# A two-layer hybrid encoder on one core: products moved from GpSimd to VectorE, later transposes and SSD matmuls, and another layer boundary

## The chip, the core and the metric

The kernel runs on one core of a Trainium2 chip. The core has five engines with queues of their own: TensorE (PE in the profile; its weight loads are PEld), VectorE (DVE), ScalarE (ACT), GpSimd (POOL) and SyncE (SP), which here only issues DMAs. The metric is the time of one execution on the device in microseconds (us), the median of the runs; lower is better.

## The reference

A sequence of 272 tokens (16 learned tokens and 256 frames) of width 2048 passes two layers, each followed by a residual and a layer norm:

```
for layer in range(2):
    f = even_mixer(h) if layer % 2 == 0 else odd_mixer(h)
    h = layer_norm(4 ** 0.25 * h + f, ln_g[layer], ln_b[layer])
```

Layer 0 projects `h` once, runs four heads of gated linear attention (GLA) and eight heads of stick-breaking attention beside each other, gates each with a Silu, and projects back. Layer 1 is a Mamba-2 mixer: a projection to z (4096), x (4096), B and C (1024 each) and dt (64); a causal convolution of four taps and a Silu over x, B and C; and per group g (8 groups of 8 heads)

```
xdt   = x * softplus(dt_raw + dt_bias)
l_mat = exp(a_cum[t] - a_cum[s]) where s <= t, else 0     # per head
cb    = C B^T                                             # per group
y     = (l_mat * cb) @ xdt + d_skip * x                   # the state between chunks included
y     = rms_norm(y * silu(z)) * norm_w
```

and a projection back. All inputs and the output are float32.

## The kernel before

Activations stand transposed: 128 features on the partitions, 272 tokens along the row, 16 such blocks (`kt`). Weights stream in as units of 1 MB (`raw`). ScalarE rounds each half unit to `whi`, an engine subtracts to get `wlo` (`split_into`, L145 to L147; VectorE, or POOL for one in six late in layer 1), and a product of float32 quality takes three matmuls: `whi` with `xhi`, `whi` with `xlo`, `wlo` with `xhi` (L165 to L167). A projection unit is 48 of them, a half unit 24. `whi` and `wlo` have five buffers of half a unit, `raw` three of a whole one; `pj` is a PSUM tile for projections (four buffers), `po` one for everything else (two), and `zb` are two fixed ones (`z`).

The mixers are Python generators ("side tasks"), which advance by one `yield` whenever the main loop ticks, four times a projection unit. That is the order in which the program is written. A list scheduler then reorders the instructions of each engine by its own estimate of times; only data dependencies hold, unless the program pins instructions. On the chip each engine runs its list in that order.

The places that the change touches:

- Stick-breaking heads (`post_sq`, `post_sk`, `post_sv`, `mix_sb`): one unit each for q, k, v of a head; the mixer is pushed at v.
- The last units of layer 0 (`out0c_unit`, c = 4 to 7), with `stat0` for each finished block of `hacc`: `xhi`/`xlo` of it times `ln_g`, and its sum and sum of squares, on POOL for blocks 0 to 13, as extra matmuls ("spare") for 14 and 15.
- `norm0`: the dt projection of 64 columns (48 matmuls into `po`), the sums over partitions by matmuls with `ones`, and mean and 1/deviation (`newton`).
- `first1`: the first six units of layer 1 (B, C, z, x, x, x of group 0) run on the rows before normalization; `fix` corrects each result by the mean and 1/deviation. Meanwhile `normalize0` normalizes `hacc`, and `residual1` transposes it into `acc` (L942, L943). After them `xhi`/`xlo` are written anew (L920, L921).
- `dt_path`: softplus of dt, the scan along the tokens (`dt_scr`, L976), a write to memory (`edr`) from which each group reloads 1.7 MB of broadcast rows (`ebc`), and transposes (`est`).
- Per group: `decay1` (M = exp of differences, L1054 to L1057; C B^T, L1069; M times it, L1080), `x_path` (Silu, transposes L1117 and L1121, times dt, `xd`), and `mix_ssd` (L1176, L1182). `silu1` clamps on VectorE (L1006), takes Exp, Ln and Exp on ScalarE (L1007 to L1009) and multiplies on POOL (L1010).
- SP's list holds the weight loads, `edr` and `ebc`, each waiting for its turn.

## Time and profile before

| | us |
|---|---|
| median of 3 runs | 1405.14 (1403.98 to 1405.44) |
| the profiled execution | 1403.88 |
| its span, first to last instruction | 1402.2 |
| PE busy | 1378.8 (98%) |
| VectorE busy | 1031.1 (74%) |
| ScalarE busy | 770.0 (55%) |
| POOL busy | 320.0 (23%) |

Layer 0 fills the span up to about 690 us. A row of the timeline gives start, length, engine, line and operation, and in brackets the idle time of the engine just before it with what ended that. A row of a group gives the busy time of all its instructions and the mean of one in ns. `L` numbers are lines of the kernel before. A fp32 matmul shows as two records.

### The profile page before, as it was taken

The numbers are of one execution on the slowest core, as the hardware profiler recorded it, in microseconds if no ns is written. First come the engines' busy times: TensorE is split into PE (matmuls) and PEld (weight loads), VectorE is DVE, ScalarE is ACT, GpSimd is POOL, SyncE is SP. The second block draws the span as 40 slices with busy tenths as digits, with TensorE's granted clock in tenths as the row PEclk, the third lists the DMA queues.
The fourth block names the chain that finished last, engine by engine and source line by source line (L and its number), as shares of the span: only waits on it lengthen the run. The fifth ranks groups of instructions, "written<-read, shape, count | busy, mean of one in ns | idle before, by whom it ended". The sixth has DMA issues, their size and how long they took to land. (4 is left out here: it accounts for less than half of the span.)

```text
span 1402.2 us, 26134 instructions
## 1 busy us (share of the span) xinstructions
PE 1378.8 (98%) x10719; PEld 1328.2 (95%) x10719; DVE 1031.1 (74%) x1669; ACT 770.0 (55%) x1144; POOL 320.0 (23%) x285
## 2 busy tenths in 40 slices
PE   9999999999999999999999999999999999999996
PEld 8999999999999999999999899899898999989985
DVE  7857575575565574558799989777887778777787
ACT  6645454354345544545587766655555655556551
POOL 0000100100101100114302325333323433424233
PEclk9999999999999999999999999999999999999998
DMA  9545444545454445443444745554646456464551
GB/s 331 178 154 171 161 160 171 172 160 179 153 179 153 153 153 194 160 153 137 151 151 172 265 170 194 202 208 162 218 157 227 176 185 225 155 210 177 193 197 61
DMA packets 37720, 249.84 MB, mean 178 GB/s; under 512 B 4256, under 2 KB 6112, under 8 KB 9184
## 3 DMA queue, kind: packets, MB, share of 16 engines
q1 hardware_dynamic: 37168, 247.77, 50.6%
q8 instruction: 84, 1.38, 0.4%
q10 hardware_dynamic: 432, 0.39, 0.1%
q14 instruction: 36, 0.29, 0.1%
HBM read 245.94 MB, written 2.20 MB: 177 GB/s over the span
## 5 line engine op out<-in xcount | busy, mean ns | idle before, releaser
L165 PE MATMUL pj<-xhi,whi 128*128 128x272 f32 (+4 forms) x2560 | 733.6, 287 | 1.1 <-ACT xhi L317 0.7
L166 PE MATMUL pj<-xlo,whi 128*128 128x272 f32 (+4 forms) x2560 | 731.1, 286 | 0.0
L167 PE MATMUL pj<-xhi,wlo 128*128 128x272 f32 (+4 forms) x2560 | 729.5, 285 | 0.0
L147 DVE TENSOR_TENSOR wlo<-raw,whi 128x1024 fp32r<-128x1024 f32 (+2 forms) x405 | 510.4, 1263 | 239.5 <-ACT whi L146 237.7
L146 ACT ACTIVATE whi<-raw 128x1024 fp32r<-128x1024 f32 (+2 forms) x435 | 449.8, 1038 | 392.5 <-PE pj L166 337.4
L165 PEld LDWEIGHTS pj<-xhi,whi 128*128 128x128 f32 x2560 | 482.2, 188 | 3.9 <-issue 1.0
L166 PEld LDWEIGHTS pj<-xlo,whi 128*128 128x128 f32 x2560 | 482.2, 188 | 1.7 <-issue 0.6
L167 PEld LDWEIGHTS pj<-xhi,wlo 128*128 128x128 f32 x2560 | 482.5, 188 | 0.8 <-issue 0.6
L165 PE MATMUL pj<-mixh,whi 128*128 128x272 f32 x384 | 110.9, 290 | 1.0 <-ACT mixh L801 1.0
L167 PE MATMUL pj<-mixh,wlo 128*128 128x272 f32 x384 | 110.4, 288 | 0.0
L166 PE MATMUL pj<-mixl,whi 128*128 128x272 f32 x384 | 110.4, 288 | 0.0
L147 POOL TENSOR_TENSOR wlo<-raw,whi 128x1024 fp32r<-128x1024 f32 x30 | 75.6, 2520 | 113.3 <-ACT whi L146 113.0
L476 PE MATMUL pj<-whi,yh 128*128 128x512 f32 (+1 forms) x244 | 94.8, 389 | 0.0
L478 PE MATMUL pj<-whi,yl 128*128 128x512 f32 (+1 forms) x244 | 94.2, 386 | 0.0
L477 PE MATMUL pj<-wlo,yh 128*128 128x512 f32 (+1 forms) x244 | 94.1, 386 | 0.0
L248 POOL TENSOR_TENSOR gr<-gr,gsc 128x1088 f32<-128x1088 f32 x6 | 15.4, 2569 | 302.1 <-ACT gsc L247 302.1
L165 PEld LDWEIGHTS pj<-mixh,whi 128*128 128x128 f32 x384 | 72.2, 188 | 1.3 <-ACT mixh L801 1.1
L166 PEld LDWEIGHTS pj<-mixl,whi 128*128 128x128 f32 x384 | 72.3, 188 | 0.2
L167 PEld LDWEIGHTS pj<-mixh,wlo 128*128 128x128 f32 x384 | 72.3, 188 | 0.1
L485 DVE SCALAR_TENSOR_TENSOR acc<-pj,rr,acc 128x512 f32<-128x512 f32 (+1 forms) x65 | 46.7, 735 | 12.1 <-PE pj L478 12.0
L478 PEld LDWEIGHTS pj<-whi,yl 128*128 128x128 f32 x244 | 45.8, 188 | 9.3
L476 PEld LDWEIGHTS pj<-whi,yh 128*128 128x128 f32 x244 | 45.8, 188 | 9.0
(327 smaller groups left out, 1527.4 us busy)
## 6 DMA issues: line engine op xcount, KB each, us to landing
raw<-in_wts SPq DMA_DIRECT2D x212, 1024.0 KB, 4.8
ebc<-edr SPq DMA_DIRECT2D x8, 1664.0 KB, 6.3
raw<-in_wts SPq DMA_DIRECT2D x9, 256.0 KB, 5.6
hacc<-in_xT SPq DMA_DIRECT2D x7, 272.0 KB, 5.7
early<-in_wts SPq DMA_DIRECT2D x2, 512.0 KB, 7.4
lg<-in_lnr SPq DMA_DIRECT2D x1, 1024.0 KB, 4.6
lb<-in_lnr SPq DMA_DIRECT2D x1, 1024.0 KB, 4.6
out_h<-acc SPq DMA_DIRECT2D x2, 512.0 KB, 2.6
```

The source lines that it names most:

```text
L146: self.nc.scalar.activation(hi, src, AF.Copy)
L147: eng.tensor_tensor(lo, src, hi.bitcast(F32), op=ALU.subtract)
L165: mm(ps, whi, xhi, start=first, stop=False)
L166: mm(ps, whi, xlo, start=False, stop=False)
L167: mm(ps, wlo, xhi, start=False, stop=last)
L248: mul(c, c, e, op=ALU.mult)
L476: mm(ps, yh[:, kk, tt], hi[:, k, :], start=kk == 0, stop=False)
L477: mm(ps, yh[:, kk, tt], lo[:, k, :], start=False, stop=False)
L478: mm(ps, yl[:, kk, tt], hi[:, k, :], start=False, stop=kk == 3)
L485: self.nc.vector.scalar_tensor_tensor(a, ps, r[:, t : t + 1], a, op0=ALU.mult, op1=ALU.add)
```

## The change

It has seven parts.

1. The mixer of a stick-breaking head is pushed at its k unit instead of its v unit; it waits for v's transposes only before the product with v.
2. The dt weights are loaded two units earlier and split one or two units earlier, into tiles of the v buffers in which high and low parts stand beside each other as 128 columns. The dt product then takes one matmul with `xhi` and one with `xlo` for each of 16 blocks, and a matmul with two stacked identities (`add2`) later sums the two halves.
3. `norm0` puts the sums of POOL ahead of the dt matmuls and the spare ones behind the tenth block, pins these on PE, subtracts the mean there (two blocks of `hacc` in one instruction), and splits the second unit of layer 1 itself. `keep_order` holds VectorE and ScalarE to the written order from the unit c = 6 to the end of `norm0`.
4. `normalize0` has only the scaling left, two blocks in one instruction. `dt_path` starts when `first1` has written `xhi`/`xlo` anew, instead of after 16 ticks.
5. The products of Silu of x (all groups) and of B and C (group 0), and all products of M with C B^T, are on VectorE; before, POOL had Silu's and two of four products of M in groups 2 to 7.
6. C B^T is held by two ticks (from group 1 on), x's transposes by five, SSD's matmuls by three, and each of these blocks is pinned on PE.
7. `split_half` skips what is already split.

The diff, cut to its core ("..." where lines are left out):

```diff
+    def keep_order(self, first):
+        ins = self.traced()
...
+        for eng in (mybir.EngineType.DVE, mybir.EngineType.Activation):
+            mine = [i for i in ins[n0:] if i.engine == eng]
+            for a, b in zip(mine, mine[1:]):
+                self.tc.add_manual_dep(b, a.name, free, reason="keep_order")
...
         if u[2] == 6:
-            self.dt_raw = self.lp.tile([P, 1024], F32, tag="gu", name="dtraw")
-            self.nc.sync.dma_start(self.dt_raw, self.wdt)
-        if u[2] == 7:
-            self.dt_parts = self.split(self.dt_raw, 1024)
+            self.first = self.traced()[-1]
+        if u[2] == 4:
+            self.dt_raw = self.lp.tile([P, 2, 8, 64], F32, tag="gu", name="dtraw")
+            self.nc.sync.dma_start(self.dt_raw.rearrange("p a k c -> p (a k c)"), self.wdt)
+        if u[2] == 5:
+            self.dt_parts = [self.lp.tile([P, 8, 2, 64], F32R, tag=n, name="dt" + n, bufs=2) for n in ("gvh", "gvl")]
+            for a, p in enumerate(self.dt_parts):
+                self.split_into(self.dt_raw[:, a], p[:, :, 0, :], p[:, :, 1, :], self.nc.vector)
...
     def post_sk(self, ps, h, j):
-        self.cur["k"] = self.sb_parts(ps, ("ke", "gk")[h % 2], 1.0)
+        k = self.sb_parts(ps, ("ke", "gk")[h % 2], 1.0)
+        v = self.cur["sv", h] = self.v_tiles(h)
+        self.mixers[4 + h // 4].append(self.push(self.mix_sb(h, self.cur["q"], k, v)))
...
     def norm0(self):
+        pin(mm(pm[:, :T], self.ones, self.ssum, start=True, stop=False))
+        pin(mm(pq[:, :T], self.ones, self.ssq, start=True, stop=False))
         for k in range(KT):
-            self.in_kt(self.ps_dt[:64, :TG], hi[:, k, :], lo[:, k, :], k, 0, TG)
...
+            if k == 10:
+                for n, (x, q) in enumerate(self.spare):
+                    l = n == len(self.spare) - 1
+                    pin(mm(pm[:, :T], self.ones, x, start=False, stop=l))
+                    pin(mm(pq[:, :T], self.ones, q, start=False, stop=l))
+            w = self.dt_parts[k // 8][:, k % 8].rearrange("p a c -> p (a c)")
+            pin(mm(self.ps_dt[:, :TG], w, self.xhi[:, k, :], start=k == 0, stop=False))
+            pin(mm(self.ps_dt[:, :TG], w, self.xlo[:, k, :], start=False, stop=k == KT - 1))
+        self.split_half(len(L0) + 1, 0)
...
+        center((0, 2))
         self.newton(rs, var, tmp)
...
+        self.split_half(len(L0) + 1, 1)
+        center(range(4, KT, 2))
+        self.keep_order(self.first)
...
     def dt_path(self, ps, scr):
-        for _ in range(16):
+        while not self.normed:
             yield
...
-    def silu1(self, v):
+    def silu1(self, v, eng=None):
-        self.nc.gpsimd.tensor_tensor(v, v, c, op=ALU.mult)
+        (eng or self.nc.gpsimd).tensor_tensor(v, v, c, op=ALU.mult)
...
     def decay1(self, g):
-        self.silu1(bc)
+        self.silu1(bc, None if g else vec)
...
+        for _ in range(2 if g else 0):
+            yield
         zb = self.zbank()
...
-            eng = nc.gpsimd if g > 1 and h in (2, 6) else vec
-            eng.tensor_tensor(M[:, h : h + 2, :], M[:, h : h + 2, :], c, op=ALU.mult)
+            vec.tensor_tensor(M[:, h : h + 2, :], M[:, h : h + 2, :], c, op=ALU.mult)
...
     def x_path(self, g, j):
-        self.silu1(xt[:, j : j + 2, :].rearrange("p a t -> p (a t)"))
+        self.silu1(xt[:, j : j + 2, :].rearrange("p a t -> p (a t)"), vec)
...
+        for _ in range(5):
+            yield
...
     def mix_ssd(self, g):
             if j == 0:
+                for _ in range(3):
+                    yield
```

How the scheduler's lists move, at three places. First PE at the end of the dt product, where `po_8046` and `po_8048` hold it and `pj_8138` and `pj_8143` are the first unit of layer 1. Before:

```order
L166 MATMUL po_8046<-xlo,whi_7976 64x274
L167 MATMUL po_8046<-xhi,wlo_7977 64x274
L165 MATMUL po_8046<-xhi,whi_7976 64x274
L848 MATMUL po_8095<-ssum,ones 128x272
L852 MATMUL po_8095<-hacc,ones 128x272
L166 MATMUL po_8046<-xlo,whi_7976 64x274
L167 MATMUL po_8046<-xhi,wlo_7977 64x274
L852 MATMUL po_8095<-hacc,ones 128x272
L165 MATMUL pj_8138<-xhi,whi_7980 128x274
```

With the change (the sums `ssum` and `ssq` stand ahead of the first dt matmul, and these rows follow the tenth block):

```order
L876 MATMUL po_8048<-xlo,dtgvl 128x274
L872 MATMUL z_64<-hacc,ones 128x272
L873 MATMUL z_65<-nsq_8029,ones 128x272
L872 MATMUL z_64<-hacc,ones 128x272
L178 MATMUL pj_8143<-xhi,whi_7982 128x274
L179 MATMUL pj_8143<-xlo,whi_7982 128x274
L180 MATMUL pj_8143<-xhi,wlo_7983 128x274
L178 MATMUL pj_8143<-xhi,whi_7982 128x274
L873 MATMUL z_65<-nsq_8046,ones 128x272
L875 MATMUL po_8048<-xhi,dtgvl 128x274
L876 MATMUL po_8048<-xlo,dtgvl 128x274
L875 MATMUL po_8048<-xhi,dtgvl 128x274
```

Block 14 and 15's `xhi` were read right behind each other at the end; now the spare sums and four rows of the next unit stand between.

Second, VectorE in group 3 around the second pair of x blocks (`xcl` is Silu's buffer, `gz` is z, `po_11355` and `po_11409` hold transposes). Before:

```order
L999 SCALAR_TENSOR_TENSOR xt_11059<-pj_11225,cpk,xt_11059 128x271
L999 SCALAR_TENSOR_TENSOR xt_11059<-pj_11225,cpk,xt_11059 128x270
L999 SCALAR_TENSOR_TENSOR xt_11059<-pj_11225,cpk,xt_11059 128x269
L1006 TENSOR_SCALAR xcl_11309<-xt_11059 128x544
L1130 TENSOR_TENSOR xd_11060<-po_11355,est 128x256 x2
L147 TENSOR_TENSOR wlo_11443<-raw_11371,whi_11442 128x1024
L147 TENSOR_TENSOR wlo_11477<-raw_11371,whi_11476 128x1024
L1130 TENSOR_TENSOR xd_11060<-po_11356,est 128x256 x2
L1136 TENSOR_TENSOR xd_8126<-z_64,est_8602 16x128 x4
```

With the change:

```order
L1044 SCALAR_TENSOR_TENSOR xt_11032<-pj_11196,cpk,xt_11032 128x271
L1044 SCALAR_TENSOR_TENSOR xt_11032<-pj_11196,cpk,xt_11032 128x270
L1044 SCALAR_TENSOR_TENSOR xt_11032<-pj_11196,cpk,xt_11032 128x269
L1051 TENSOR_SCALAR xcl_11282<-xt_11032 128x544
L160 TENSOR_TENSOR wlo_11394<-raw_11330,whi_11393 128x1024
L1055 TENSOR_TENSOR xt_11032<-xt_11032,xcl_11282 128x544
L160 TENSOR_TENSOR wlo_11444<-raw_11330,whi_11443 128x1024
L160 TENSOR_TENSOR wlo_11482<-raw_11390,whi_11481 128x1024
L1051 TENSOR_SCALAR xcl_11423<-gz_11328 128x512
L1180 TENSOR_TENSOR xd_11033<-po_11409,est 128x256 x2
L1180 TENSOR_TENSOR xd_11033<-po_11410,est 128x256 x2
L1186 TENSOR_TENSOR xd_8126<-z_64,est_8751 16x128 x4
```

The product of Silu now stands in VectorE's list behind its clamp and one weight split.

At the same place PE: before, the second pair's transposes stand 98 rows behind the end of the last x unit, one row into a z unit.

```order
L165 MATMUL pj_11373<-xhi,whi_11327 128x256
L166 MATMUL pj_11373<-xlo,whi_11327 128x256
L167 MATMUL pj_11373<-xhi,wlo_11328 128x256
L165 MATMUL pj_11441<-xhi,whi_11374 128x256
L1117 MATMUL po_11356<-ident,xt_11059 128x128 x4
L1121 MATMUL z_64<-ident,xt_11059 16x128 x2
L166 MATMUL pj_11441<-xlo,whi_11374 128x256
L167 MATMUL pj_11441<-xhi,wlo_11375 128x256
```

With the change, both pairs' stand together, 108 rows behind it:

```order
L179 MATMUL pj_11392<-xlo,whi_11333 128x256
L180 MATMUL pj_11392<-xhi,wlo_11334 128x256
L1167 MATMUL po_11409<-ident,xt_11032 128x128 x4
L1167 MATMUL po_11410<-ident,xt_11032 128x128 x4
L1171 MATMUL z_64<-ident,xt_11032 16x128 x4
L178 MATMUL pj_11392<-xhi,whi_11333 128x256
L179 MATMUL pj_11392<-xlo,whi_11333 128x256
```

The first pair's transposes have moved by one z unit. In groups 2, 4, 5, 6 and 7 the second pair's now stand 157, 125, 117, 109 and 125 rows behind that unit.

Third, PE at the first SSD matmuls of group 0 (`M_8677` and `M_8820` are M, `pj` x units of group 1). Before:

```order
L166 MATMUL pj_9238<-xlo,whi_9160 128x272
L1176 MATMUL po_9086<-M_8677,xd_8510 64x256 x2
L167 MATMUL pj_9238<-xhi,wlo_9161 128x272
L165 MATMUL pj_9238<-xhi,whi_9160 128x272
L166 MATMUL pj_9238<-xlo,whi_9160 128x272
L167 MATMUL pj_9238<-xhi,wlo_9161 128x272
L165 MATMUL pj_9238<-xhi,whi_9160 128x272
L166 MATMUL pj_9238<-xlo,whi_9160 128x272
L167 MATMUL pj_9238<-xhi,wlo_9161 128x272
L165 MATMUL pj_9238<-xhi,whi_9160 128x272
L1176 MATMUL po_9086<-M_8677,xd_8510 64x256 x2
L1176 MATMUL po_9086<-M_8677,xd_8510 64x144 x4
```

With the change:

```order
L178 MATMUL pj_9282<-xhi,whi_9246 128x272
L1167 MATMUL po_8951<-ident,xt_8482 128x128 x4
L1171 MATMUL z_64<-ident,xt_8482 16x128 x4
L1229 MATMUL po_9125<-M_8820,xd_8483 64x256 x4
L179 MATMUL pj_9282<-xlo,whi_9246 128x272
L180 MATMUL pj_9282<-xhi,wlo_9247 128x272
L178 MATMUL pj_9282<-xhi,whi_9246 128x272
```

Before they stand in the first x unit of group 1, in five pieces; now in the second, behind the transposes of the second pair, in two pieces.

## The prediction

> **What bounds the kernel now.** I read the page's first part, then PE's waits, then the timelines around them.

> ```profile
> span 1402.2 us, 26134 instructions
> ...
> PE 1378.8 (98%) x10719; PEld 1328.2 (95%) x10719; DVE 1031.1 (74%) x1669; ACT 770.0 (55%) x1144; POOL 320.0 (23%) x285
> ```

> PE is busy for all but 23 us, and part of that lies at the two ends of the program. So only two things can shorten the span: less work on PE, or fewer of PE's waits. All its waits are these nine:

> ```profile
> engine line waited for: us in total, times, longest us
> PE po L1117 <- POOL xt L1010: 4.4, 6, 1.1
> PE po L1176 <- DVE M L1080: 1.9, 1, 1.9
> PE po L165 <- ACT xhi L815: 1.3, 2, 0.7
> PE po L942 <- ACT acc L943: 1.2, 1, 1.2
> PE po L227 <- POOL b_one L217: 1.1, 1, 1.1
> PE pj L165 <- ACT mixh L801: 1.0, 1, 1.0
> PE pj L165 <- ACT xhi L317: 0.7, 1, 0.7
> PE pj L165 <- DVE fix L900: 0.3, 1, 0.3
> PE po L166 <- DVE xlo L816: 0.2, 1, 0.2
> ```

> Two of them (L227, L317: 1.8 us) belong to the start, which is left alone. The other seven, 10.3 us, all stand where the edits are. One costs more than its length. PE's timeline at the wait of 1.9 us (start, length, instruction), and three stretches of 1 us behind it (length, busy time of PE, PEld, DVE, ACT and POOL, granted clock of PE, DMA share, GB/s):

> ```profile
> 772.42 0.88 PE L1176 MATMUL po<-M,xd 128*64 128x256 f32 x4 [1.87 <-DVE M L1080]
> ...
> 774.08 0.43 PE L167 MATMUL pj<-xhi,wlo 128*128 128x272 f32 x1
> 774.30 0.43 PE L165 MATMUL pj<-xhi,whi 128*128 128x272 f32 x1
> ...
> 773.00:774.00 1.00, 1.00 (x5) 0.77 (x4) 1.00 (x2) 0.97 (x2) 0.00 (x0) 0.50 0.99 359
> 774.00:775.00 1.00, 1.00 (x7) 1.00 (x5) 1.00 (x3) 1.00 (x2) 0.00 (x0) 0.50 0.98 359
> ...
> 776.00:777.00 1.00, 1.00 (x13) 0.67 (x10) 1.00 (x3) 0.35 (x2) 0.77 (x1) 0.94 0.97 393
> ```

> PE looks busy there, but two projection matmuls start 0.22 us apart (774.08, 774.30), where 0.13 is usual (680.34 and 680.47, below). The granted clock tells why: it is 0.50 from about 772.7 to 776.7, and 4 us at half speed lose 2.0 us. This wait therefore costs 3.9 us.

> **The change part by part.** The profiled execution took 1403.9 us with its span of 1402.2; the median of the runs is 1405.1, so 1.2 us is added at the end. I call 680.34, where PE starts the dt matmuls, the boundary.

> ```profile
> 680.34 0.29 PE L165 MATMUL po<-xhi,whi 128*64 128x274 f32 x1
> 680.47 0.29 PE L166 MATMUL po<-xlo,whi 128*64 128x274 f32 x1
> ...
> 684.20 1.21 DVE L147 TENSOR_TENSOR wlo<-raw,whi 128x1024 fp32r<-128x1024 f32 x1
> 685.33 0.77 DVE L462 TENSOR_TENSOR hacc<-hacc,pj 128x272 f32<-128x272 f32 x2
> ...
> 688.68 0.62 PE L852 MATMUL po<-hacc,ones 128*128 128x272 f32 x2
> ...
> 695.42 0.43 DVE L860 SCALAR_TENSOR_TENSOR var<-po,ntmp 128x272 f32<-128x272 f32 x1
> ...
> 751.69 1.14 DVE L976 TENSOR_TENSOR_SCAN dt_scr<-dt_scr 64x272 f32<-64x272 f32 x3
> ...
> 758.38 1.60 DVE L1006 TENSOR_SCALAR xcl<-xt 128x544 f32<-128x544 f32 x1
> ...
> 764.60 0.94 DVE L1054 TENSOR_SCALAR M<-ebc,est 128x256 f32<-128x256 f32 x1 [2.48 <-DMA ebc<-edr]
> ```

> *Stick-breaking from the k unit.* The last head's values matmuls end 28 PE rows before the first matmul that reads its `mixh`, against none before: 28 x 0.125 = 3.5 us, over two operations of some 0.45 us each. Of 1.0 I take 0.9.

> *The boundary's waits.* The last two additions to `hacc` (L462) run at 685.33 though their matmuls ended by 680.3: VectorE is in order and has weight splits ahead of them (684.20). That makes `xhi` and `xlo` late, 1.5 us in all. Now the addition and `xlo` of both blocks stand together, with the dt split moved ahead, and PE has the two sums and 20 dt matmuls (3 us) before it needs them. The spare matmuls follow in the middle. All of the 1.5 goes.

> *The dt product.* 48 matmuls become 32, and starts are 0.125 apart (680.34, 680.47): -2.0. The sum over the two halves is one fp32 matmul, which PE runs as two passes (L852 at 688.68: two in 0.62, each 0.39 long, so 0.23 apart): +0.5. Net -1.5.

> *VectorE from the boundary on.* It is full there, so it decides how much of PE's gain remains. Unit prices (mean of one; starts in a row are 0.07 to 0.1 closer):

> ```profile
> L147 DVE TENSOR_TENSOR wlo<-raw,whi 128x1024 fp32r<-128x1024 f32 x390 | 502.0, 1289 | 237.2 <-ACT whi L146 235.7 <-issue 0.2
> ...
> L927 DVE TENSOR_TENSOR hacc<-hacc,z 128x272 f32<-128x272 f32 x16 | 5.7, 422 | 0.0
> ...
> L1006 DVE TENSOR_SCALAR xcl<-xt 128x544 f32<-128x544 f32 x16 | 9.4, 588 | 0.2
> ...
> L385 DVE SCALAR_TENSOR_TENSOR hacc<-hacc,shiftc 128x544 f32<-128x544 f32 x8 | 5.2, 719 | 0.0
> ...
> L318 DVE TENSOR_TENSOR xlo<-hacc,xhi 128x544 fp32r<-128x544 f32 x7 | 4.9, 723 | 0.0
> ```

> From L860 to the end of the scans VectorE needed 57.4 us (695.42 to 752.83). The rows of the change between the same two instructions: 16 centring and scaling operations of 544 columns instead of 32 of 272 (5.2/8 each against 5.7/16: -1.0), one weight split more (+1.1), seven convolution and two fix operations fewer at some 0.4 each, one small sum more (-3.3). That gives 54.2. `var` can start 5.3 us after the boundary (PE's sums and dt matmuls, then two ScalarE copies), so the scans end at 59.5. Walking PE's rows the same way (dt and sums 5.9; units of 48 at 0.12 to 0.13; transposes 0.11 each), it reaches the transposes of the scan at 59.4. The same addition for the two transposes of group 0's x: PE 83 and 95, VectorE 80.9 and 92.1, where both silu products of x (0.65 each) and that of B now lie on VectorE. VectorE is level or 2 to 3 us ahead, but collisions with POOL can eat that (L1006 at 758.38 took 1.60, where its mean is 0.59). No wait of M is left: M ends 10 us before PE asks, as the reload of `ebc` (2.48 us of waiting at 764.60) starts after 62 with no weights ahead of it in SP's queue.

> So the wait at L1176 with its half clock (3.9) goes, and up to 0.8 us comes back at the scan's or x's transposes: I take 3.1 (bounds 0 to 3.9). Of the waits at the residual's transposes and at L900 (1.5) I take 0.8 (0 to 1.5): ScalarE has the same row of copies there, and PE arrives earlier.

> [...]

> *Groups 2 to 7.* Six times PE waits for x's silu product on POOL. In group 3, and as groups:

> ```profile
> L1010 POOL TENSOR_TENSOR xt<-xt,xcl 128x544 f32<-128x544 f32 x16 | 24.9, 1557 | 86.5 <-ACT xcl L1009 86.5
> ...
> L1080 POOL TENSOR_TENSOR M<-M,cb 128x800 f32<-128x800 f32 x12 | 28.8, 2420 | 0.0
> ...
> L1080 DVE TENSOR_TENSOR M<-M,cb 128x800 f32<-128x800 f32 x20 | 37.2, 1894 | 6.8 <-POOL cb L236 6.7
> ...
> 772.54 0.97 DVE L1080 TENSOR_TENSOR M<-M,cb 128x800 f32<-128x800 f32 x1
> ...
> 960.53 1.04 DVE L1006 TENSOR_SCALAR xcl<-xt 128x544 f32<-128x544 f32 x1
> ...
> 964.16 0.65 ACT L1009 ACTIVATE xcl<-xcl 128x544 f32<-128x544 f32 x1
> ...
> 964.89 1.58 POOL L1010 TENSOR_TENSOR xt<-xt,xcl 128x544 f32<-128x544 f32 x1 [3.62 <-ACT xcl L1009]
> ```

> The product costs 0.72 on VectorE (as L318) instead of 1.56, and the second pair's transposes stand 108 to 157 PE rows behind the last x unit instead of 98 in group 3: 1 to 7 us more room. M's products cost 0.97 when POOL has none beside them, so four on VectorE take 3.9 us, where two took 3.8 (2 x 1.894) with POOL's 4.8 behind them. VectorE gets 16 x 0.72 of silu and loses about that by fewer collisions; it stays near its 74% of the span, and that is cover enough, since it idles 235.7 us in waits for `whi`. Of 4.4 I take 4.0. What comes next is the transposes of `xd`, 110 PE rows before the SSD matmuls: 13 us, no wait. Held SSD rows end long before the output units two groups later.

> *Pins.* SSD of group 0 goes in two pieces instead of five. At a return the first two projection starts lose some 0.1 us each: 0.4 (0 to 0.9).

> Sum: 0.9 + 1.5 + 1.5 + 3.1 + 0.8 + 4.0 + 0.4 = 12.2. 1403.9 - 12.2 + 1.2 = **1393 us**.

> **The rivals.**
> *A, VectorE swallows the boundary.* If its queue runs some 10 us later than I added up at x's second transposes, PE waits 7 us there and the terms from the boundary's waits to the residual's (6.9) are lost: 1393 + 6.9 = 1400. For it: VectorE has no slack here,

> ```profile
> 700.00:760.00 60.00, 58.45 (x481) 57.44 (x481) 59.89 (x131) 46.90 (x84) 5.38 (x5) 1.00 0.44 154
> ```

> Against: the addition by the same prices gives the old trace's 57.4 to 0.1. Chance 0.15.
> *B, the six waits stay,* because the transposes of groups 3 and 6 move by only some 10 rows, and the product now queues behind a weight split: 1397. Against: ScalarE's last exponential no longer stands behind VectorE's late clamp. Chance 0.12.
> *C, one new wait of 1.9 us or more* halves the clock again: 1393 + 3.9 = 1397. Likeliest at x's first transposes. Chance 0.10.
> *D, slower: VectorE blocked in order.* The product stands directly behind its clamp in groups 4 and 7, so VectorE idles through three ScalarE steps (about 2 us) while splits queue. A half unit is 24 matmuls, 3 us, and a split 1.3, so PE waits only if splits are less than 2 us ahead; at 14 such places it would be up to 28 us, 1409 if half of it shows. It decides from 0.9 us a place (12.2/14). Against: splits wait for PE (235.7 us on `whi`), not the reverse. Chance 0.05. [...]

> **How the numbers follow.** The forecast has 0.58. All gains whole give 14.7: 1390.5. My range is 1390 to 1400, which leaves out some 0.05 below, A with B together (gain 5.3 - 4.0 = 1.3: no change, 0.06 taken from A and B) and D. About 0.2%, 2.8 us, is what can be told here: faster 0.89, same 0.06, slower 0.05.

> **What would show it.** In the new profile PE's waits should be under 4 us in all, with none on POOL's `xt`, none on M, none on `xhi` behind the stick-breaking output, and the granted clock 1.00 from 700 to 800. Waits at the scan's or x's transposes of 1 to 2 us would show VectorE level with PE (my margin), 4 us and more rival A. The dt matmuls should be 32, 0.125 apart. It is wrong if PE waits on `wlo`, or if waits on `xt` merely change their engine.

## The result, and the profile after

| | before | with the change |
|---|---|---|
| median of six runs, us | 1404.9 | 1394.2 |
| lowest to highest, us | 1403.98 to 1405.44 | 1393.15 to 1394.98 |
| span of the profiled execution, us | 1402.2 | 1392.3 |

The ratio of the times is 0.9923, 95% interval 0.9913 to 0.9934: 10.7 us faster. The forecast was 1393, with a range of 1390 to 1400.

The page of the changed kernel, its first rows:

```profile
span 1392.3 us, 26070 instructions
...
PE 1376.1 (99%) x10705; PEld 1327.7 (95%) x10705; DVE 1014.6 (73%) x1684; ACT 771.3 (55%) x1146; POOL 261.9 (19%) x256
```

All of PE's waits in the changed kernel (line waited at, what was waited for, us in total, times, longest):

```profile
PE pj L178 <- DVE fix L935: 2.0, 1, 2.0
PE po L240 <- POOL b_one L230: 1.1, 1, 1.1
PE pj L178 <- ACT xhi L330: 0.6, 1, 0.6
PE z L867 <- POOL ssq L857: 0.4, 1, 0.4
PE pj L178 <- ACT whi L159: 0.4, 2, 0.2
PE po L987 <- ACT acc L988: 0.3, 1, 0.3
```

The span is 9.9 us shorter. PE's waits fell from 12.1 us to 4.8, which is 7.3, and its busy time from 1378.8 to 1376.1, which is 2.7: together 10.0. Gone are the waits for `mixh` (1.0), for `xhi` and `xlo` at the boundary (1.5), for M (1.9) and for x's Silu product (4.4). The wait at the residual's transposes shrank from 1.2 to 0.3. New are 0.4 for a sum of squares on GpSimd, 0.4 for rounded weights at the program's start, and one that no step of the prediction has: 2.0 us for a `fix`, the operation that takes an early layer-1 unit out of its `pj` tile in PSUM (a buffer for such a tile is called a bank below) and applies the norm. In PE's timeline of the changed kernel:

```profile
734.60 0.28 PE L180 MATMUL pj<-xhi,wlo 128*128 128x272 f32 x1
736.86 0.38 PE L178 MATMUL pj<-xhi,whi 128*128 128x256 f32 x1 [1.97 <-DVE fix L935]
...
737.20 0.28 PE L180 MATMUL pj<-xhi,wlo 128*128 128x256 f32 x1
737.31 0.28 PE L178 MATMUL pj<-xhi,whi 128*128 128x256 f32 x1
...
738.41 0.42 PE L178 MATMUL pj<-xhi,whi 128*128 128x256 f32 x1
738.62 0.42 PE L179 MATMUL pj<-xlo,whi 128*128 128x256 f32 x1
```

and stretches behind it (length, busy us of PE, PEld, DVE, ACT, POOL, granted clock, DMA share, GB/s):

```profile
738.00:739.00 1.00, 1.00 (x8) 1.00 (x7) 1.00 (x2) 0.00 (x0) 0.00 (x0) 0.66 0.72 270
739.00:740.00 1.00, 1.00 (x7) 1.00 (x6) 1.00 (x4) 0.24 (x1) 0.00 (x0) 0.50 1.04 442
740.00:741.00 1.00, 1.00 (x7) 1.00 (x7) 1.00 (x4) 1.00 (x3) 0.00 (x0) 0.50 0.50 205
741.00:742.00 1.00, 1.00 (x7) 1.00 (x7) 1.00 (x4) 1.00 (x3) 0.00 (x0) 0.63 0.00 0
```

The wait brings the half clock that the wait for M had brought before. The clock is 0.50 for 3.4 us (0.68 + 1 + 1 + 0.74 of the four stretches). Starts are 0.21 apart there (738.41, 738.62) instead of 0.12 (737.20, 737.31), so some 1.5 us are lost (an estimate: 3.4 x (1 - 0.12/0.21)). VectorE and ScalarE at the same place:

```profile
733.42 0.42 ACT L1196 ACTIVATE gz<-fix 128x256 f32<-128x256 f32 x1
```

```profile
733.63 1.21 DVE L160 TENSOR_TENSOR wlo<-raw,whi 128x1024 fp32r<-128x1024 f32 x1
734.77 0.42 DVE L1013 SCALAR_TENSOR_TENSOR dt_scr<-dt_scr 64x272 f32<-64x272 f32 x1
...
735.19 1.20 DVE L160 TENSOR_TENSOR wlo<-raw,whi 128x1024 fp32r<-128x1024 f32 x1
736.32 0.48 DVE L935 SCALAR_TENSOR_TENSOR fix<-dt_scr,uv,pj 128x272 f32<-128x272 f32 x1
```

PE has four `pj` banks. The unit that it wants to begin at 734.9 takes the bank of the unit four earlier, whose `fix` starts only at 736.32. That `fix` writes into one of two buffers `yu`, and the one that it gets is free when ScalarE's copy of the z unit ends, at 733.84. VectorE, in order and without a gap, has two weight splits and a step of the dt chain in front of it then.

On VectorE the products came out nearly as priced (groups by line in the changed kernel):

```profile
L1127 DVE TENSOR_TENSOR M<-M,cb 128x800 f32<-128x800 f32 x32 | 29.8, 984 | 4.4 <-POOL cb L249 4.4
L1055 DVE TENSOR_TENSOR xt<-xt,xcl 128x544 f32<-128x544 f32 x16 | 12.4, 775 | 12.0 <-ACT xcl L1054 11.9
```

M's 32 products cost 0.98 each, all on VectorE: 29.8 us, less than the 37.2 that 20 of them cost there before.

### The profile page after: what moved, and what is told of

It reads as the page before. It is cut to its first block, busy times and chain, and to the rows that moved or that the text cites. A ratio compares the mean times of both kernels' runs of the same rounds, so it can differ in the third digit from the quotient of the medians.

```text
span 1392.3 us, 26070 instructions
## 1 busy us (share of the span) xinstructions
PE 1376.1 (99%) x10705; PEld 1327.7 (95%) x10705; DVE 1014.6 (73%) x1684; ACT 771.3 (55%) x1146; POOL 261.9 (19%) x256
## 4 chain that ended last, share of the span: by engine, by line
PE 94%; ACT 2%; DVE 2%; DMA 1%; POOL 1%; issue 0%; ACTq 0%; SPq 0%
PE pj L179 25%; PE pj L178 25%; PE pj L180 25%; PE pj L494 4%; PE pj L496 4%; PE pj L495 4%; PE po L1229 2%; PE po L608 1%; ACT whi L159 1%; DVE wlo L160 1%; ACT hacc L975 1%; DVE xlo L836 1%; PE po L1167 1%; DMA raw<-in_wts 0%; PE z L1117 0%
## 5 line engine op out<-in xcount | busy, mean ns | idle before, releaser
L180 PE MATMUL pj<-xhi,wlo 128*128 128x272 f32 (+4 forms) x2560 | 730.9, 286 | 0.0
L160 DVE TENSOR_TENSOR wlo<-raw,whi 128x1024 fp32r<-128x1024 f32 (+2 forms) x405 | 504.5, 1249 | 249.2 <-ACT whi L159 244.9
```

Of the source, the lines that this page charges most:

```text
L160: eng.tensor_tensor(lo, src, hi.bitcast(F32), op=ALU.subtract)
L180: mm(ps, wlo, xhi, start=False, stop=last)
```

## The experiments

Twelve kernels were run. The first three each make a part of the change alone, on the kernel before.

**The stick-breaking mixer alone.**

```diff
     def post_sk(self, ps, h, j):
-        self.cur["k"] = self.sb_parts(ps, ("ke", "gk")[h % 2], 1.0)
+        k = self.sb_parts(ps, ("ke", "gk")[h % 2], 1.0)
+        v = self.cur["sv", h] = self.v_tiles(h)
+        self.mixers[4 + h // 4].append(self.push(self.mix_sb(h, self.cur["q"], k, v)))
```

> The kernel before with the stick-breaking mixer started from the k unit, and nothing else of the change. My theory: the wait of 1.0 us for mixh goes and PE reaches the boundary 1 us earlier, so 1404.9 - 1.0 = 1403.9. Rival (the boundary swallows it): VectorE is full at the boundary, so PE only waits 1.0 us longer there for xhi, xlo and the products of M: 1404.9, with the wait of mixh gone and the waits for xhi and M longer by 1 us together.

Measured: 1402.7 (ratio 0.9985, 0.9977 to 0.9994), 2.3 us less. PE's waits at the boundary and in group 0:

```profile
PE po L1204 <- POOL ysq L1198: 1.2, 1, 1.2
...
PE po L165 <- ACT xhi L817: 1.0, 2, 0.7
...
PE po L1178 <- DVE xd L1132: 0.6, 1, 0.6
```

The wait for `mixh` is gone and the boundary does not swallow it: `xhi` costs 1.0 instead of 1.3. The wait for M is gone too, and 1.8 us for `ysq` (the sums of squares of y, on GpSimd) and `xd` stand in its place. The half clock is still there in this profile, but among the residual's transposes (0.50 from 731 to 734). Where the gain beyond 1.0 us comes from was not settled.

**The boundary alone.** Only the hunks on the dt weights, `norm0`, `first1`, `normalize0`, `dt_path` and `split_half`:

```diff
-        for _ in range(16):
+        while not self.normed:
             yield
...
+            pin(mm(self.ps_dt[:, :TG], w, self.xhi[:, k, :], start=k == 0, stop=False))
+            pin(mm(self.ps_dt[:, :TG], w, self.xlo[:, k, :], start=False, stop=k == KT - 1))
```

> The kernel before with the new boundary alone (dt weights earlier and as one product of 32 matmuls, pinned sums, the late dt chain); Silu, M products, holds and mixers as before. My theory, from the trace after: dt product 1.5, boundary waits 1.5, residual's waits 1.2 and the wait for M with its half clock 3.9 go, and a new wait of 2 us for a fix comes with a half clock of 2 us: 1404.9 - 8.1 + 4.0 = 1400.8. Rival A (VectorE swallows all of it): 1404.9 - 1.5 = 1403.4 or later. Rival C' (the new wait needs the Silu product of B on VectorE as well, so it is not there): 1396.8.

Measured: 1402.9 (0.9983, 0.9974 to 0.9992), with single times from 1400.5 to 1404.4. PE's waits, the ones behind the boundary:

```profile
PE pj L178 <- DVE fix L933: 2.0, 1, 2.0
PE po L1245 <- POOL ysq L1239: 1.9, 1, 1.9
...
PE z L1164 <- POOL xt L1053: 0.6, 1, 0.6
```

The wait for M is gone, with room: M's last product ends at 768.0 and PE asks for it at 781.5. But 2.0 us came for the `fix` on VectorE, and 2.5 for `xt` of group 1 and for `ysq` of group 0, both on GpSimd, where that product (802.5 to 804.9) stands directly ahead of the sums. So PE's waits come to 12.2 us, where they were 12.1, and the boundary alone gains 2.1 us, little more than its shorter product. That lies nearer to rival A's 1403.4 than to my 1400.8, but only the 2.0 us for the `fix` are of A's kind; VectorE's queue did not swallow the rest. And the wait for the `fix` belongs to the new boundary: it does not need B's Silu product on VectorE.

**Silu, M products and holds alone.**

```diff
-        self.silu1(xt[:, j : j + 2, :].rearrange("p a t -> p (a t)"))
+        self.silu1(xt[:, j : j + 2, :].rearrange("p a t -> p (a t)"), vec)
...
+        for _ in range(5):
+            yield
...
+                for _ in range(3):
+                    yield
```

> The kernel before with the Silu products of x (and of group 0's B and C) and all M products on VectorE, and the three holds with their pins; boundary and mixers as before. My theory: the six waits for x's Silu product (4.4) go, and the pins give some 0.1 us a group: 1404.9 - 5 = 1399.9, while the wait for M in group 0 with its half clock stays or grows (VectorE has 2 us more there: 1 to 2 us later). Rival (the parts only work together): the wait for M grows so much that less than 2 us is left: 1403 or later.

Measured: 1397.0 (0.9941, 0.9928 to 0.9955), 8.0 us less. Both theories said less. All six waits for `xt` are gone, and so is the wait for M with its half clock, although VectorE's chain at the boundary is the old one. The new waits are short, one for B and C of group 1 and one at group 0's SSD:

```profile
PE z L1072 <- POOL bc L1010: 0.9, 1, 0.9
...
PE po L1184 <- DVE mt L1062: 0.3, 1, 0.3
```

M's first product ends at 776.1 here, 3.9 us later than before (772.3), but PE starts SSD of group 0 at 776.3, later by as much: its rows stand later in its list. The hold of three ticks and its pins are the part of the edit that aims at this; they were not tried apart. The three parts alone gain 2.3 + 2.1 + 8.0 = 12.4, against 10.7 together. In each the wait for M disappears, and it can be lost only once; that this is the whole difference was not shown.

**Silu back on GpSimd**, in the changed kernel:

```diff
-        self.silu1(xt[:, j : j + 2, :].rearrange("p a t -> p (a t)"), vec)
+        self.silu1(xt[:, j : j + 2, :].rearrange("p a t -> p (a t)"))
...
-        self.silu1(bc, None if g else vec)
+        self.silu1(bc)
```

> The changed kernel with the Silu products of x and of group 0's B and C back on GpSimd; holds, pins and M products as in the change. Theory 'the engine': the product's 0.8 us more and GpSimd's queue were the six waits, so most of 4.4 comes back: 1397 to 1398.6, with PE waiting six times for xt from GpSimd. Rival 'the room': the hold of five ticks alone covers the slower product: 1394.2 within 0.5, without such waits.

Measured: 1401.1 (0.9972, 0.9960 to 0.9983), 6.9 us more than the change. Neither theory has it. No wait for `xt` came back in groups 1 to 7, so the room alone is enough there. What it lost is one wait in group 0:

```profile
PE po L1167 <- POOL xt L1055: 5.3, 1, 5.3
```

GpSimd's row, and VectorE's beside it:

```profile
759.18 8.12 POOL L1055 TENSOR_TENSOR xt<-xt,xcl 128x544 f32<-128x544 f32 x1 [2.15 <-ACT xcl L1054]
```

```profile
759.25 1.88 DVE L1127 TENSOR_TENSOR M<-M,cb 128x800 f32<-128x800 f32 x2
...
761.61 1.21 DVE L160 TENSOR_TENSOR wlo<-raw,whi 128x1024 fp32r<-128x1024 f32 x1
762.74 1.87 DVE L1127 TENSOR_TENSOR M<-M,cb 128x800 f32<-128x800 f32 x2
764.54 1.21 DVE L160 TENSOR_TENSOR wlo<-raw,whi 128x1024 fp32r<-128x1024 f32 x1
```

One product took 8.12 us on GpSimd, where the mean of x's had been 1.56. It ended at 767.3, 1.6 us after VectorE's last split (764.54 + 1.21 = 765.75). VectorE's products kept their 0.94 and its splits their 1.21 meanwhile. The wait also brought the half clock for two times 3.4 us (0.50 in the stretch from 765 to 768, 0.56 from 768 to 772):

```profile
765.00:768.00 3.00, 0.65 (x3) 0.65 (x4) 1.76 (x6) 0.00 (x0) 2.30 (x1) 0.50 0.64 262
```

**No holds**, in the changed kernel (engines and pins stay):

```diff
-        for _ in range(2 if g else 0):
-            yield
...
-        for _ in range(5):
-            yield
...
-                for _ in range(3):
-                    yield
```

> The changed kernel without the three holds (two ticks before C B^T, five before the transposes of x, three before SSD); pins and engines as in the change. The run with Silu on GpSimd showed that the holds cover the slower product in groups 1 to 7. Theory 'room': VectorE's product alone, 0.8 us faster, is not enough where the wait was 0.5 to 1.4 us, since it also queues behind weight splits: some of the six waits come back under another engine's name, 2 to 3 us, and SSD of group 0 waits for M or xd again, 1 to 4 us with a half clock: 1397 to 1401. Theory 'engine' (mine in the prediction, by halves): 0.8 us of six waits of 0.5 to 1.1 us is most of them, and group 0 is no worse: 1394.2 to 1395.5.

Measured: 1395.2 (0.9931, 0.9918 to 0.9943). That is 1.0 us more than the change took in another session, which the two intervals do not tell apart. Waits for `xt` come to 0.3 us in all:

```profile
PE po L1163 <- DVE xt L1055: 0.3, 1, 0.3
```

So "engine" is right: VectorE's product alone removes the six waits. With the run before it, either of the two is enough in groups 1 to 7, and neither could be called the cause. In group 0 the engine is needed.

**Two M products of groups 2 to 7 back on GpSimd**, in the changed kernel:

```diff
-            vec.tensor_tensor(M[:, h : h + 2, :], M[:, h : h + 2, :], c, op=ALU.mult)
+            eng = nc.gpsimd if g > 1 and h in (2, 6) else vec
+            eng.tensor_tensor(M[:, h : h + 2, :], M[:, h : h + 2, :], c, op=ALU.mult)
```

> The changed kernel with two of the four M products of groups 2 to 7 back on GpSimd. Both holds and engine cover the six waits singly, so M's engine should not matter while the holds stand: theory 'covered': 1394.2 within 0.7. Theory 'collisions': GpSimd's M products slow VectorE's splits and products (2.7 to 6.0 us for M beside them, 0.97 alone), and SSD's M comes late: 1395 to 1397, with PE's waits on M or xd in groups 2 to 7.

Measured: 1397.9 (0.9952, 0.9940 to 0.9965), against 1393.8 for the change in the same session: 4.1 us lost. Of the two, "collisions" is nearer, but PE does not wait for M or `xd`:

```profile
PE po L1168 <- DVE xt L1055: 4.0, 4, 1.5
```

The old waits are back under VectorE's name. The longest of them, on VectorE and on GpSimd:

```profile
1045.04 2.47 DVE L1055 TENSOR_TENSOR xt<-xt,xcl 128x544 f32<-128x544 f32 x1 [1.88 <-ACT xcl L1054]
```

```profile
1044.54 2.39 POOL L160 TENSOR_TENSOR wlo<-raw,whi 128x1024 fp32r<-128x1024 f32 x1 [10.98 <-ACT whi L159]
```

Beside a split on GpSimd x's product took 2.47 instead of 0.72. So it did in group 7 (2.46), and these two groups have 2.7 of the 4.0 us. In group 2, with 1.1 us, the product takes its 0.72; there the transposes of the second pair now stand directly behind those of the first (874.2 and 877.7, where the change has 874.8 and 880.6), so PE asks earlier. GpSimd's M products do not run beside x's product at any of the three; how they bring the waits about was not followed further. That the waits "merely change their engine" was named as a sign of failure; it takes GpSimd's M products to bring it about.

**Where the wait for the `fix` comes from.** Two edits of the changed kernel, alone and together. The first lets the z unit's `fix` write into z's own tile, so that it needs no `yu` buffer and no copy:

```diff
-            self.post(u, fix(ps, P, t0))
+            if u[2] == "z":
+                self.cur["z", 0] = lp.tile([P, 4, S], F32, tag="gz", name=self.nm("gz"))
+            self.post(u, fix(ps, P, t0, self.cur["z", 0][:, 0, :] if u[2] == "z" else None))
```

> The changed kernel, but the fix of group 0's z unit writes its result straight into z's tile, without the buffer yu and the copy on ScalarE. Theory 'buffer': the wait of 2.0 us for a fix, and its half clock of 2 us, come from the two yu buffers: the fix that frees PE's bank could not start before z's copy on ScalarE had freed one (its row moves 14 rows up in VectorE's order): up to 4 us less, 1390.2, if nothing else is late. Theory 'VectorE is full': the fixes behind it come late in turn, since VectorE has the same work: PE waits 1 to 2 us at the next two units instead, 1392 to 1395.

The second takes three weight splits off VectorE:

```diff
-            pool = h == 1 and n >= 24 and n % 3 == 0
+            pool = h == 1 and (n in (4, 5, 6) or n >= 24 and n % 3 == 0)
```

> The changed kernel with the second weight split of three units of the boundary (the 5th to 7th of layer 1) on GpSimd, which is idle there. Theory 'VectorE is full': 3.4 us less on VectorE between 700 and 730, so the fix comes in time, the wait of 2.0 us and the half clock go: 1390.2 to 1391.5. Theory 'buffer': the fix still waits for z's copy, so the wait only shrinks with ScalarE's and VectorE's earlier start, by 0 to 1 us: 1393 to 1394.2; slower if splits on GpSimd (2.6 us each) hold VectorE's up.

> Both edits: z's fix in place and three splits on GpSimd. If either theory alone explains the wait, this is no better than the better of the two runs. If the buffer and the full VectorE each keep part of it, this alone reaches 1390 (1394.2 less 2.0 of waiting and 2.0 of half clock).

Measured, in one session: 1391.7 (0.9910, 0.9895 to 0.9925), 1391.7 (0.9907, 0.9894 to 0.9921) and, both together, 1389.9 (0.9895, 0.9882 to 0.9909); the change took 1394.2 in another session. With the first edit these two waits are left behind the boundary's sums, the second of them in group 0's SSD:

```profile
PE pj L178 <- ACT gz L1199: 1.3, 1, 1.3
PE po L1258 <- POOL ysq L1252: 1.2, 1, 1.2
```

With the second, and VectorE's row of the `fix`:

```profile
PE pj L178 <- DVE fix L935: 0.9, 1, 0.9
PE pj L179 <- DVE xlo L964: 0.8, 1, 0.8
```

```profile
736.68 0.48 DVE L935 SCALAR_TENSOR_TENSOR fix<-dt_scr,uv,pj 128x272 f32<-128x272 f32 x1
```

With z in place the `fix` starts at 724.4, 12 us earlier: the buffer made it late. PE's list changes with it (the next two units are interleaved), and behind them PE waits 1.3 us for another bank. This one is freed by ScalarE's copy of a z unit (`gz`), not by VectorE. With the splits moved the `fix` starts no earlier (736.7, where the change has 736.3). The wait falls to 0.9 because PE comes to it 1.4 us later, having first waited 0.8 for an `xlo` (until 730.9) and done the scan's transposes (735.3). In neither profile does the clock halve (mean granted clock 0.997 and 0.998, where the change's profile has 0.996). With both edits no wait is left between the boundary's sums and group 0's `ysq` (1.1 us). So the buffer is shown as a cause of the late `fix`. That VectorE's full queue is another is not: fewer splits help, alone and with the buffer gone, but what they change for the wait on `gz` was not followed.

**The best version.** Both edits, and group 0's sums of squares of y on VectorE:

```diff
-                nc.gpsimd.tensor_tensor(sq, sq, s2, op=ALU.add)
+                (nc.gpsimd if g else vec).tensor_tensor(sq, sq, s2, op=ALU.add)
```

> Both edits of the run before (z's fix in place, three splits on GpSimd) and, in group 0, the sums of squares of y on VectorE instead of GpSimd. PE's last wait in group 0, 1.1 us for these sums, goes, since GpSimd took 0.9 to 1.6 us for each and VectorE takes some 0.35: 1389.9 - 1.1 = 1388.8. Rival (VectorE has no room in group 0): the sums queue behind splits and another wait of 1 us comes: 1389.9.

Measured: 1388.35 (0.9888 of the kernel before, 0.9873 to 0.9903), 5.4 us less than the change in the same session. The wait for `ysq` is gone and no other came:

```profile
PE po L240 <- POOL b_one L230: 1.1, 1, 1.1
...
PE z L867 <- POOL ssq L857: 0.4, 1, 0.4
```

**The clock.** A probe, run once, whose time says nothing of the kernel, and the change once more:

```diff
+                for m in range(96 + 7 * n % 29):
+                    pin(nc.tensor.matmul(ps[:, :W], ws[m % 2], b, start=True, stop=True))
...
+                vec.tensor_copy(t[:, :64], ps[:, :64])
+                vec.tensor_tensor(u[:, :k], raw[:, :k], t[:, :1].broadcast_to([P, k]), op=ALU.mult)
+                vec.tensor_tensor(c, raw[:, :W], u[:, k - 1 : k].broadcast_to([P, W]), op=ALU.mult)
```

> Not the kernel but a probe that leaves the whole computation out: 80 streams of 97 to 125 matmuls of PE (as the projections', 128x128 by 272), and before each stream PE waits for three operations of VectorE, of which the middle one has eight lengths, so that the waits are some 1.0, 1.2, 1.4, 1.6, 1.8, 2.0, 2.4 and 2.9 us long, ten of each at different places of the clock's grid. Theory 'grid' (from five traces: half clock came for 3.41 us, always at a multiple of 3.413 us from the first full clock, where the grid interval before it had held 1.58 us or more of waiting, and not where it had 1.55 or less; one of 1.73 had none): a wait halves the clock only by what of it lies within one interval; 1.0 and 1.2 never do, 1.8 and 2.0 do in some half of their places, 2.9 in most. Theory 'length' (as the prediction priced it): every wait of 1.9 us or more halves the clock for about 4 us, and none below. [...]

> The changed kernel once more, as the base for the other runs of this call: 1394.2, with the wait of 2.0 us for a fix. By theory 'grid' the half clock behind it comes in some executions and not in others, since the wait can fall across a boundary of the grid: times spread over some 2 us; by theory 'length' it is there in each.

Two waits of the probe, both 1.94 us long, in PE's timeline:

```profile
87.13 0.36 PE L34 MATMUL ps<-c,w 128*128 128x272 f32 x1 [1.94 <-DVE c L42]
...
171.11 0.36 PE L34 MATMUL ps<-c,w 128*128 128x272 f32 x1 [1.94 <-DVE c L42]
```

and the stretches behind them (the sixth number is the granted clock):

```profile
87.00:89.00 2.00, 1.87 (x15) 1.90 (x16) 0.00 (x0) 0.00 (x0) 1.00 0.00 0
89.00:91.00 2.00, 2.00 (x18) 2.00 (x18) 0.00 (x0) 0.00 (x0) 1.00 0.00 0
...
173.00:175.00 2.00, 2.00 (x11) 2.00 (x11) 0.00 (x0) 0.00 (x0) 0.50 0.00 0
```

The first wait leaves the clock at 1.00, the second halves it. From the trace's clock records I laid a grid of 3.4133 us from the first full clock (7.95). The 3.4133 come from the profile before the change: its half clock begins 768.00 us after the first full clock, which is 225 x 3.4133, and its record is 3.413 long. The first wait, 85.19 to 87.13, has 1.27 us on one side of a grid point (86.46) and 0.67 on the other; the second, 169.16 to 171.11, lies within one interval, and the half clock begins where that ends, at 171.79 (granted clock 0.70 from 171 to 173). Over the 79 waits:

| length, us | waits | halved the clock |
|---|---|---|
| 1.0 to 1.7 | 40 | 0 |
| 1.9 | 10 | 6 |
| 2.1 | 10 | 7 |
| 2.5 | 9 | 8 |
| 3.1 | 10 | 7 |

## Why the prediction was right, and where not

**What bounds the kernel.** Right: PE's waits and its work explain the whole gain (7.3 + 2.7 of 9.9).

**Stick-breaking, 0.9.** The wait of 1.0 is gone. The first run alone shows that nothing takes its place at the boundary.

**Boundary's waits, 1.5.** The waits for `xhi` and `xlo` are gone, but 0.4 us for the sum of squares on GpSimd is new, since PE now asks for it first: 1.1.

**The dt product, 1.5.** 32 matmuls at 0.127 take 4.1 us where 48 took 6.0, and two records of 0.42 each for the halves' sum come on top. Of PE's 2.7 us less this is some 1.5. The other 1.2, where I took 0.4 for the pins, was not tried apart.

**Group 0's SSD, 3.1.** This is the step that failed, in what it let come back. That the wait for M goes was right, and for the reason given. In the changed kernel M's last product ends 16 us before PE asks for it (forecast: 10):

```profile
763.06 0.98 DVE L1127 TENSOR_TENSOR M<-M,cb 128x800 f32<-128x800 f32 x1
```

```profile
780.34 1.08 PE L1229 MATMUL po<-M,xd 128*64 128x256 f32 x8
```

With the boundary alone it is 13 us. The third run shows that the wait can also go without that chain, though there M is ready only 0.2 us ahead. What comes back is another matter. I compared VectorE with PE only where PE reads data, at the scan's and x's transposes, and took "up to 0.8 us". There it was right: no wait at either, with VectorE 1.8 to 2.6 us ahead. But PE also waits for PSUM banks, and a `fix` that frees one was 2.0 us late, with the half clock behind it. The term was 1.9 + 1.5 gained and 2.0 + 1.5 lost: nothing, the lower of the bounds given. The row of the prediction that shows VectorE without slack had a part of the cause; the walk left out the banks, and with them the two buffers that hold a `fix` back.

**Residual, 0.8.** Of 1.5 there, 1.2 is gone.

**Six waits, 4.0.** All 4.4 are gone. The prediction gave two reasons, the faster product and the room. Each is enough without the other in groups 1 to 7, and a third, M's products off GpSimd, turned out to be needed with them: without it 4.0 us return.

**The sum.** Taken were 12.2. Measured between the two profiles were 9.9: 1.0, 1.1, 1.5, 0, 1.2, 4.4 and the 1.2 on PE make 10.4, less some 0.3 of longer waits at the program's start and the rounding of the terms. The missing 3.1 of group 0 were made up in part by terms taken too low (1.3 on balance), so the time came out 1.2 us above 1393. That it came so near is in this part luck: the errors have opposite signs.

**The rivals.** A did not happen: at x's second transposes PE waits for nothing. The boundary alone gains as little as A says, but mostly for other reasons. B did not happen. C happened in its mechanism, one new wait of about 2 us with a half clock, at a place that it did not name; its price is 3.5, not 3.9, as the half clock lasted 3.4 us and cost 1.5 (the estimate above). The wait for M, which the prediction priced at 3.9 too, had cost 3.4 for the same reason (0.50 from 772.7 to 776.1). D did not happen: PE waits for no `wlo`. (Its 1409 should be 1407 by its own numbers, 1393 + 14.)

**The signs.** Waits on PE of 4.8 us are over the 4 that were named, and the clock from 700 to 800 is not 1.00; the rest (no wait on `xt`, M or `xhi` at the boundary, 32 dt matmuls) is as forecast.

## What to carry to other kernels

When PE gets earlier, walk along everything that it waits for: not only the data that it reads, but the PSUM banks and the buffers that an evacuation needs before it can free one (2.0 us for a `fix` here). Where two edits both remove a wait, test each without the other before naming a cause, and where three parts each remove the same wait, do not add up their gains. Look at what runs beside a piece of work on VectorE before moving it to GpSimd: here a product on GpSimd took 8.12 us beside VectorE's products and splits back to back, where the mean had been 1.56, and a product on VectorE took 2.47 beside a split on GpSimd instead of 0.72.

## What the runs showed of the hardware

**The half clocks of these traces lie on a grid of 3.41 us.** In the probe the granted clock was 0.50 for one interval behind each wait of which 1.92 us or more lay in the interval before (28 of 79 waits; behind one of them for two), and behind none with 1.86 or less. Behind the wait of 5.3 us with Silu back on GpSimd it was 0.50 for two. In the kernels' profiles before and with the change, too, the half clock behind the wait begins a whole number of such intervals after the first full clock: 768.00 us or 225 intervals before (4.71 to 772.71), 733.87 us or 215 with the change (4.46 to 738.32). So a wait of 2.0 us for the `fix` cost 2.0 in one execution and 3.5 in another (2.0 + the 1.5 estimated above): in the profile of the boundary alone the same wait left the clock at 1.00,

```profile
736.00:738.00 2.00, 0.12 (x1) 0.13 (x2) 2.00 (x5) 1.32 (x2) 0.00 (x0) 1.00 0.00 0
738.00:740.00 2.00, 2.00 (x18) 2.00 (x19) 1.99 (x5) 0.00 (x0) 0.00 (x0) 1.00 0.71 213
```

as it would with a grid point inside the wait; where that point lay is not shown. In the kernels the limit is less sharp than in the probe: with the stick-breaking mixer alone PE idled 1.58 us from 728 to 731, among the residual's transposes (its waits there are 1.3 for `acc` and 0.3 for a `fix`), and the clock was 0.50 from 731 to 734. What else counts there stays open.

**One product on GpSimd took 8.12 us.** It ran beside back-to-back products and splits of VectorE, which were not slowed (0.94 and 1.21 each). This was seen once. The product ended 1.6 us, one product's usual length (1.56), behind the last of VectorE's four products and two splits. That it got no turn between them is my guess from these times; no run shows the cause. In the run with M products on GpSimd it was VectorE's product that took longer: 2.47 us, begun at 1045.04 behind a split of GpSimd that began at 1044.54, and it ended 0.6 us after that split. The end of the 8.12 us has a second sign: VectorE's next operation waited for the product until 767.33.
